# Sum of squared differences by rows: 16 loads in place of 18, larger last pieces of row 7, and that row's squares and sums in PSUM

## The chip, the cores and the metric

The kernel runs on one core of a Trainium2 chip. The metric is the device time of one execution in microseconds; lower is better. A trace is of one execution; the times are medians of several.

## The reference

```python
batch, dim = 1024, 4096
x = np.random.randn(batch, dim).astype(np.float32)
y = np.random.randn(batch, dim).astype(np.float32)

def reference(x, y, axis):          # axis = -1
    return np.sum((x - y) ** 2, axis=axis).astype(np.float32)
```

Two inputs of 16.8 MB each are read once, and 4 KB are written. Each of the 128 partitions holds eight rows of 4096 columns ("row 0" to "row 7"), 32768 columns of x and as many of y.

## The kernel before

The sync engine issues all loads. VectorE subtracts y from x in place, ScalarE squares each piece and sums it in the same instruction, and a small VectorE reduction adds the partial sums of a row. Tensors live in one of two on-chip memories, SBUF (`alloc_sbuf_tensor`) or PSUM (`alloc_psum_tensor`); the kernel before uses SBUF alone. The lists `xw` and `yw` are the widths of the loads, in columns.

```python
xw = [4096, 12288, 8192, 5472, 1280, 960, 320, 160]
yw = [16256, 8192, 2624, 2784, 1344, 480, 480, 288]
late, last = 128, 192          # the last 192 columns of y, then 128 columns of row 3, loaded last of all
LATE = 3
halved = (1, 2, 3, 4)          # pieces of these loads of y are computed in two halves
...
for j, (c0, c1) in enumerate(ys):
    final = j == len(ys) - 1
    wait_loaded(c1, landed_y[j][1])
    for piece in pieces_of(j, c0, c1):
        sub(*piece)                                     # VectorE
        if final:                                       # the late piece of row 3, wholly on VectorE
            nc.vector.tensor_tensor_reduce(..., scalar=parts_of(r, 1), accum_out=results[:, r : r + 1])
            continue
        square(*piece, where[piece])                    # ScalarE, with accum_out
    if j == 4:
        for r in (4, 5, 6):
            complete(r)
complete(7)                                             # VectorE: waits for the last sum of row 7, adds 8 sums
nc.sync.dma_start(out=ov, in_=results)
...
def square(c0, c1, acc):
    a = X[:, home(c0, c1)]
    nc.scalar.wait_ge(diffs, n["diffs"])
    nc.scalar.activation(out=a, in_=a, func=Square, accum_out=acc).then_inc(acts, 1)
```

The first five loads (49024 columns of x and y together) fill the buffers; the other 13 are issued when row 1 has been squared, at 53.4 us, and queue behind them. A square is two instructions on ScalarE: the activation, and an accumulator read that writes the sum.

## Time and profile before

| kernel before | |
|---|---|
| median of 6 runs | 84.18 us (84.02 to 84.40) |
| span of the profiled run | 82.6 us |
| last load landed | 80.25 us |
| store of the results issued | 81.18 us |

All positions below are microseconds from the start of the profiled span. "Landing" is the moment at which a load's semaphore has its last increment; the trace records it.

The final reduction alone, from the groups by form, and the end of VectorE's timeline (start, duration, what):

```profile
L188 DVE TENSOR_REDUCE results<-parts 128x1 f32<-128x8 f32 x1 | 0.2, 161 | 0.0
...
80.95 0.08 DVE L204 DVE_READ_ACCUMULATOR2_ANT results<- 128x1 f32 x1
80.99 0.16 DVE L188 TENSOR_REDUCE results<-parts 128x1 f32<-128x8 f32 x1
```

### The profile page before, as it was taken

What the parts mean: (1) busy time and instruction counts of PE and PEld (TensorE: products, weight loads), DVE (VectorE), ACT (ScalarE), POOL (GpSimd) and SP (SyncE); (2) the same over time, 40 slices, a digit from 0 to 9 for tenths busy, and PEclk for the clock granted to TensorE, in tenths of its full rate; (3) what the DMA queues carried; (4) which work ended last, traced back from release to release, by engine and by line L of the source; (5) the groups of instructions that cost most, each with busy time, mean ns of one, the idle gap of its engine ahead of it and who ended that gap; (6) DMA issues with size and microseconds to landing.
All of it is one profiled execution on the core that took longest, in us unless ns stands there. A gap on an engine that the chain in (4) does not pass through costs nothing.

```text
span 82.6 us, 136 instructions
## 1 busy us (share of the span) xinstructions
DVE 36.8 (45%) x27; ACT 33.4 (40%) x41; POOL 0.2 (0%) x4
## 2 busy tenths in 40 slices
DVE  0000000000000000000299999999189996989992
ACT  3300000000000000000000979889896999899991
POOL 0000000000000000000000000000000000000000
DMA  5998998888999991999599699969979799999960
GB/s 127 389 500 381 595 547 381 381 381 381 504 504 504 504 504 63 441 504 504 254 508 508 286 476 508 476 286 508 423 339 509 339 437 440 426 402 416 395 220 2
DMA packets 2736, 33.56 MB, mean 406 GB/s; under 512 B 432, under 2 KB 1328, under 8 KB 1712
## 3 DMA queue, kind: packets, MB, share of 16 engines
q1 hardware_dynamic: 2736, 33.56, 95.9%
HBM read 33.55 MB, written 0.00 MB: 406 GB/s over the span
## 4 chain that ended last, share of the span: by engine, by line
DMA 63%; SPq 16%; DVE 12%; ACT 4%; issue 1%
DMA Y<-in_y_dram 63%; SPq L108 16%; DVE X L175 11%; ACT X L181 4%; DVE Y L204 0%; DVE results L188 0%; SPq L220 0%; DVE results L204 0%
## 5 line engine op out<-in xcount | busy, mean ns | idle before, releaser
L175 DVE TENSOR_TENSOR X<-X,Y 128x2048 f32<-128x2048 f32 (+10 forms) x21 | 36.2, 1780 | 44.3 <-DMA Y<-in_y_dram 44.3
L181 ACT ACTIVATE X<-X 128x2048 f32<-128x2048 f32 (+9 forms) x20 | 31.2, 1559 | 46.1 <-DVE X L175 46.0
L181 ACT ACTIVATION_READ_ACCUMULATOR X<-X 128x1 f32 x20 | 3.7, 186 | 0.0
L181 ACT ACT_TABLE_LOAD x1 | 1.3, 1283 | 1.4 <-PEq L19 1.4
L188 DVE TENSOR_REDUCE results<-parts 128x1 f32<-128x2 f32 (+2 forms) x4 | 0.4, 152 | 0.0
L204 DVE CUSTOM_DVE_ANT_0 Y<-X,parts 128x128 f32<-128x128 f32 x1 | 0.4, 352 | 0.0
L250 POOL MEMSET const-bfloat16-1.0<- 128x1 bf16 x1 | 0.1, 101 | 0.0
L250 POOL MEMSET const-uint8-127<- 128x1 uint8 x1 | 0.1, 101 | 0.0
L250 POOL MEMSET const-float32-0.0<- 128x1 f32 x1 | 0.1, 98 | 0.2 <-issue 0.2
L250 POOL MEMSET const-float32-1.0<- 128x1 f32 x1 | 0.1, 98 | 0.0
L204 DVE DVE_READ_ACCUMULATOR2_ANT results<- 128x1 f32 x1 | 0.1, 83 | 0.0
## 6 DMA issues: line engine op xcount, KB each, us to landing
Y<-in_y_dram SPq DMA_DIRECT2D x1, 8128.0 KB, 39.0
X<-in_x_dram SPq DMA_DIRECT2D x1, 6144.0 KB, 20.2
X<-in_x_dram SPq DMA_DIRECT2D x1, 4096.0 KB, 48.3
Y<-in_y_dram SPq DMA_DIRECT2D x1, 4096.0 KB, 57.5
X<-in_x_dram SPq DMA_DIRECT2D x1, 2736.0 KB, 13.3
X<-in_x_dram SPq DMA_DIRECT2D x1, 2048.0 KB, 7.1
Y<-in_y_dram SPq DMA_DIRECT2D x1, 1392.0 KB, 19.0
Y<-in_y_dram SPq DMA_DIRECT2D x1, 1312.0 KB, 16.1
```

What stands on the lines that cost most here:

```text
L108: nc.sync.dma_start(out=dst[:, home(c0, c1)], in_=src[:, c0:c1]).then_inc(sem, 16)
L175: nc.vector.tensor_sub(out=a, in0=a, in1=Y[:, home(c0, c1)]).then_inc(diffs, 1)
L181: nc.scalar.activation(out=a, in_=a, func=Square, accum_out=acc).then_inc(acts, 1)
L188: nc.vector.tensor_reduce(out=results[:, r : r + 1], in_=parts_of(r, len(row_parts[r])), axis=mybir.AxisListType.X, op=add,).then_inc(sums, 1)
L204: nc.vector.tensor_tensor_reduce(out=Y[:, home(*piece)], in0=X[:, home(*piece)], in1=X[:, home(*piece)], scale=1.0, scalar=parts_of(r, 1), ...
L250: nc = _bacc.Bacc("TRN2", target_bir_lowering=False, num_devices=1)
```

## The change

The intent: fewer loads, so fewer packets; larger last pieces; and, so that ScalarE can keep up with them, the squares of row 7 (which nobody reads) and its eight sums in PSUM. Five of the six lists and numbers change (`LATE` stays), and the outputs of ScalarE in row 7.

```diff
-    xw = [4096, 12288, 8192, 5472, 1280, 960, 320, 160]
-    yw = [16256, 8192, 2624, 2784, 1344, 480, 480, 288]
-    late, last = 128, 192
+    xw = [4096, 12288, 8192, 5536, 1344, 736, 576]
+    yw = [16288, 8192, 2720, 2816, 1344, 736, 288]
+    late, last = 96, 288
     LATE = 3
-    halved = (1, 2, 3, 4)
+    halved = (1, 2, 3, 4, 5)
...
+    last_parts = nc.alloc_psum_tensor("last_parts", [P, 512], F32).ap()
+    last_squares = nc.alloc_psum_tensor("last_squares", [P, 7 * 512], F32).ap()
+    squares_at = {}
+    k = 0
+    for piece in reversed(row_parts[-1]):
+        w = piece[1] - piece[0]
+        if k + w > 7 * 512:
+            break
+        squares_at[piece] = last_squares[:, k : k + w]
+        k += w
...
     def parts_of(r, m):
-        return parts[:, first[r] : first[r] + m]
+        home_of = last_parts if r == R - 1 else parts
+        return home_of[:, first[r] : first[r] + m]
...
     def square(c0, c1, acc):
...
-        nc.scalar.activation(out=a, in_=a, func=Square, accum_out=acc).then_inc(acts, 1)
+        to = squares_at.get((c0, c1), a)
+        nc.scalar.activation(out=to, in_=a, func=Square, accum_out=acc).then_inc(acts, 1)
```

More of the change, by code (lines that the diff above doesn't have):

```diff
@@ L145 @@
     parts = nc.alloc_sbuf_tensor("parts", [P, total], F32).ap()
+    last_parts = nc.alloc_psum_tensor("last_parts", [P, 512], F32).ap()
+    last_squares = nc.alloc_psum_tensor("last_squares", [P, 7 * 512], F32).ap()
+    squares_at = {}
     k = 0
-    for r, p in enumerate(row_parts):
-        for piece in p:
-            where[piece] = parts[:, k : k + 1] if len(p) > 1 else results[:, r : r + 1]
-            k += len(p) > 1
+    for piece in reversed(row_parts[-1]):
[4 more added lines that the diff above has]
+        k += w
     first = {}
@@ L154 @@
         if len(p) > 1:
-            first[r] = k
-            k += len(p)
+            first[r] = 0 if r == R - 1 else k
+            k += 0 if r == R - 1 else len(p)
     def parts_of(r, m):
-        return parts[:, first[r] : first[r] + m]
+        home_of = last_parts if r == R - 1 else parts
+        return home_of[:, first[r] : first[r] + m]
+    for r, p in enumerate(row_parts):
+        for k, piece in enumerate(p):
+            where[piece] = parts_of(r, len(p))[:, k : k + 1] if len(p) > 1 else results[:, r : r + 1]
     seen_x = [0]
```

## The prediction

> **What bounds the kernel now.** I read the page from the top: busy shares first, then the slices, then the chain, and then the trace in order of time for the last five microseconds.
>
> ```profile
> DVE 36.8 (45%) x27; ACT 33.4 (40%) x41; POOL 0.2 (0%) x4
> ...
> DMA  5998998888999991999599699969979799999960
> ```
>
> Neither engine is busy half of the span, while the DMA row is near full until its last two slices. The transfers bound the kernel, but "DMA-bound" says only when the last bytes land. What follows that landing is the other part of the time.
>
> ```profile
> 66.94 13.12 DMA Y<-in_y_dram
> 80.05 0.02 issue
> 80.08 0.57 DVE X L175 x2
> 80.65 0.03 issue
> 80.67 0.35 DVE Y L204
> 81.03 0.01 DVE results L204
> 81.03 0.12 DVE results L188
> ```
>
> This is the end of the chain that ended last (start, duration, what). The load of the last 192 columns of y lands at 80.05 us. Then come two subtractions (192 and 128 columns), the fused multiply-and-sum of the late 128 columns, and the final reduction. The store is issued at about 81.18 and the span is 82.6. So there are three clocks in the tail: the stream (80.05), VectorE (1.1 us behind it), and ScalarE, which the chain hides. ScalarE's own timeline:
>
> ```profile
> 78.88 0.60 ACT L181 ACTIVATE X<-X 128x480 f32<-128x480 f32 x1
> 79.38 0.19 ACT L181 ACTIVATION_READ_ACCUMULATOR X<-X 128x1 f32 x1
> 79.47 0.59 ACT L181 ACTIVATE X<-X 128x480 f32<-128x480 f32 x1
> 79.97 0.19 ACT L181 ACTIVATION_READ_ACCUMULATOR X<-X 128x1 f32 x1
> 80.08 0.44 ACT L181 ACTIVATE X<-X 128x288 f32<-128x288 f32 x1
> 80.42 0.19 ACT L181 ACTIVATION_READ_ACCUMULATOR X<-X 128x1 f32 x1
> 80.52 0.35 ACT L181 ACTIVATE X<-X 128x192 f32<-128x192 f32 x1
> 80.77 0.19 ACT L181 ACTIVATION_READ_ACCUMULATOR X<-X 128x1 f32 x1
> ```
>
> There is no gap in brackets: ScalarE runs back to back from about 72.9 us to the end. Its last sum is out at 80.77 + 0.19 = 80.96, and the final reduction, which needs it, starts at 80.99. VectorE is free for that reduction at the same 80.99 (accumulator read from 80.95). The two compute engines are **tied** at the end, so a change has to shorten both, or the stream, to win anything.
>
> **What the Trainium skill says.** "DMA: Bandwidth & Descriptors", Specifications, gives a fabric ceiling of 435 GB/s and asks for at least 512 B per transfer for line rate. The first load lands at 7.1 us and the fifth at 60.27 (issue 2.77 + 57.5 to landing). Between them lie 12288 + 16256 + 8192 + 8192 = 44928 columns of 512 B in 53.17 us: 1.183 ns a column, 433 GB/s. The trace agrees; this stream has nothing left to gain but per-load costs. "ScalarE: Activation LUTs", What ACT_TABLE_LOAD costs, gives 186 ns + 0.833 ns per column for an ACTIVATE with immediate operands; the rows above agree (0.60 us at 480, 0.35 at 192). The same page (What happens when an `exp` ACTIVATE runs) calls PSUM the lower-latency port for ScalarE, without a figure. "Perfetto Trace Analysis", Optimizing Scalar/DVE Operations, has it: a data-access overhead of about 93 ns for ScalarE on SBUF against 51 on PSUM, and about 60 against 125 for VectorE, with the write half overlapping the next instruction. No instruction of the kernel before touches PSUM, so this trace can't confirm it. The cited sentence about overlap is what decides this case.
>
> **The change part by part.**
>
> *Stream.* All bytes stay. The 13 loads after the fifth carry 16512 columns, 19.54 us at 1.183 ns, but need 80.2 - 60.27 = 19.97 us (the last 128-column load is issued at 67.4 and takes 12.8). The rest is about 0.033 us for each load. Two loads fewer save 0.07 us. The new final load has 96 columns, 384 B per partition, below the skill's 512 B; it is one load, and I charge nothing beyond the usual for it. The fifth load comes 32 columns later, 0.04 us. Laying the new sizes one after another gives landings of 76.7 (y 1344), 78.5 (y 736), 79.2 (x 576), 79.6 (y 288), 80.0 (y 288) and 80.15 (y 96): the stream ends some 0.07 us sooner, but the load before the last comes at nearly the same time as before.
>
> *VectorE.* From the trace, a subtraction takes 0.155 us + 1.042 ns a column and the next one starts about 0.08 before its end. After 80.0: 288 columns (the next starts 0.375 later), 96 columns (0.255 to its end), 0.03 for the wait, 0.24 to the accumulator read, 0.04 to the reduction: it can start at about 80.97. Before it was 80.99. The tail subtracts 384 columns instead of 320, but multiplies 96 instead of 128. **Nothing won**, about 0.02.
>
> *ScalarE.* Start to start, a square costs 0.20 us + 0.833 ns a column: activation to accumulator read 0.11, read to next activation 0.09. Row 7 had eight squares (640, 672, 672, 672, 480, 480, 288, 192) and still has eight (704, 736, 672, 672, 352, 384, 288, 288), the same 4096 columns. The number of instructions in the tail does not fall; fewer loads are offset by halving the 736 piece. But the last square is now 288 and not 192 wide, 0.08 us longer. I replayed both kernels with these durations, each engine waiting for landings and for the other engine. The replay puts the store of before at 81.19 (measured 81.18). With the new sizes and everything still in SBUF, ScalarE's backlog grows: its last sum comes at about 81.27, the reduction at 81.30, the store at 81.49, that is **0.30 us later**. So the sizes alone lose, and PSUM is there to pay for them.
>
> *PSUM.* Seven of the eight squares of row 7 write their squares there (3392 columns fit in 7 x 512; the first 704 do not), and all eight write their sums there. If the 42 ns (93 - 51) come off start to start, seven squares gain 0.29 us; as ScalarE then catches up and waits for VectorE at the last piece, about 0.27 is felt and the last sum comes at 80.94 to 80.97: level with VectorE, store at 81.17. If the accumulator read gains too, it is off the path by then, and VectorE's 80.97 is the floor. If only the acknowledgement gets shorter and start to start stays, 42 ns once at the end are all: store at 81.45. Last, the final reduction now reads eight sums from PSUM: by the skill up to 65 ns more than the 0.161 us of today. Sum: 84.19 + (81.17 - 81.18) + 0.06 = 84.24 in the good case; 84.19 + 0.27 + 0.06 = 84.5 in the bad one.
>
> **The rivals.** (1) *PSUM does not speed up the chain of squares*: for it, the skill's remark that the write half overlaps, and the 0.09 us overlap seen between every activation and its accumulator read; against it, the 0.11 us from the end of an activation's columns to the accumulator read, which reads no tensor and so looks like a cost of the destination. Time 84.5. I give it 0.4. (2) *PSUM gives the 42 ns or more*: ScalarE stops being tied, VectorE and the stream alone set the end; 84.15 to 84.25. I give it 0.5. (3) *The stream gains more than counted*, because larger packets run better: a view of 1328 packets under 2 KB speaks for it, but per-load costs add up to only 0.43 us in all 13 loads, and half of it would be needed for even 0.2 us. With VectorE in step, 84.0. I give it 0.1. (4) *The 384 B load is slow, or ScalarE's and VectorE's accesses to PSUM get in each other's way.* Against the second: "PSUM — Partial Sum Buffer", PSUM bank collisions, says two engines on one bank at once give an error, not a delay, and here VectorE reads the sums only after ScalarE's last. A slow last load has a slack of 0.25 us, since the 288 subtraction covers it.
>
> **Range and chances.** The two main cases are 84.2 and 84.5; I put the median at 84.25. The runs of before spread from 84.17 to 84.4, so the range is 84.0 to 84.6. All that this change can touch is the last microsecond of 84; 2% is 1.7 us. Chances: faster by over 2%: 0.01, same 0.98, slower 0.01.
>
> **What would show each step.** Landings: the last load at 80.1 to 80.2, with no gap in the DMA row. ScalarE: for an activation into PSUM, a duration near 0.187 + 0.833 ns per column less 42 ns, and, what counts, the distance from one start to the next at equal width (0.20 + 0.833 ns per column today). A small idle time before the 288-column squares would confirm the good case; back-to-back squares to the end with a last sum after 81.2, the bad one. The final reduction: 0.16 against up to 0.23 us. The prediction is wrong if squares into PSUM are slower, if a write across two banks costs extra, or if the stream itself moves by more than 0.2 us.

## More of the kernel before

From the page's parts on DMA and on groups of instructions (line, engine, operation, out<-in, count, then busy time in us and the mean ns of one, then idle time before):

```profile
DMA packets 2736, 33.56 MB, mean 406 GB/s; under 512 B 432, under 2 KB 1328, under 8 KB 1712
...
L181 ACT ACTIVATION_READ_ACCUMULATOR X<-X 128x1 f32 x20 | 3.7, 186 | 0.0
```

## The result, and the profile after

| | before | changed |
|---|---|---|
| median of 6 runs, us | 84.18 | 84.10 (83.99 to 84.39) |
| changed / before | | 0.9995, 95% interval 0.9972 to 1.0018 |
| fifth load landed, us | 60.27 | 60.33 |
| last load landed, us | 80.25 | 80.19 |
| store issued, us | 81.18 | 81.28 |
| span, us | 82.6 | 82.7 |

A ratio is the mean time of one kernel's fast runs over that of the other's fast runs of the same rounds, so it is not quite the ratio of the medians in the table. The two kernels are the same in time. The loads end 0.06 us sooner, and the store leaves 0.10 us later: something in the tail takes back more than the stream gives.

The page of the changed kernel, the same rows as before:

```profile
DVE 36.8 (44%) x27; ACT 33.2 (40%) x41; POOL 0.2 (0%) x4
...
DMA  5999998888999995599699889969989899999950
...
DMA packets 2448, 33.56 MB, mean 406 GB/s; under 512 B 528, under 2 KB 784, under 8 KB 1424
...
L193 ACT ACTIVATION_READ_ACCUMULATOR last_squares<-X 128x1 f32 x7 | 0.9, 129 | 0.0
L200 DVE TENSOR_REDUCE results<-last_parts 128x1 f32<-128x8 f32 x1 | 0.2, 167 | 0.0
```

There are 288 packets fewer and the DMA row is as full as it was. An accumulator read takes 129 ns in place of 186 at the seven squares that go to PSUM (149 at the first square of row 7, whose sum alone goes there). The final reduction, which now reads PSUM, takes 167 ns against 161 before.

The end of the chain that ended last (start, duration, what):

```profile
57.31 22.36 DMA Y<-in_y_dram
79.67 0.02 issue
79.69 0.47 DVE X L186
80.16 0.02 issue
80.19 0.88 ACT last_squares L193 x4
81.06 0.02 issue
81.09 0.17 DVE results L200
```

This is a different chain from that of before. It does not start at the load before the last (landed at 80.03) but one load earlier, at 79.67: 288 columns of y, their subtraction, and then **both** last squares on ScalarE, one after the other. VectorE is done with the late piece before that, as its timeline shows:

```profile
80.72 0.32 DVE L216 CUSTOM_DVE_ANT_0 Y<-X,parts 128x96 f32<-128x96 f32 x1
80.97 0.08 DVE L216 DVE_READ_ACCUMULATOR2_ANT results<- 128x1 f32 x1
81.09 0.17 DVE L200 TENSOR_REDUCE results<-last_parts 128x1 f32<-128x8 f32 x1
```

VectorE reads its accumulator at 80.97 and could reduce soon after; the reduction starts at 81.09, when ScalarE's last sum is there. ScalarE's timeline:

```profile
76.13 0.77 ACT L193 ACTIVATE X<-X 128x704 f32<-128x704 f32 x1
76.81 0.15 ACT L193 ACTIVATION_READ_ACCUMULATOR X<-X 128x1 f32 x1
76.86 0.77 ACT L193 ACTIVATE last_squares<-X 128x736 f32<-128x736 f32 x1
77.57 0.13 ACT L193 ACTIVATION_READ_ACCUMULATOR last_squares<-X 128x1 f32 x1
77.62 0.73 ACT L193 ACTIVATE last_squares<-X 128x672 f32<-128x672 f32 x1
...
80.19 0.41 ACT L193 ACTIVATE last_squares<-X 128x288 f32<-128x288 f32 x1
80.53 0.13 ACT L193 ACTIVATION_READ_ACCUMULATOR last_squares<-X 128x1 f32 x1
80.59 0.41 ACT L193 ACTIVATE last_squares<-X 128x288 f32<-128x288 f32 x1
80.92 0.14 ACT L193 ACTIVATION_READ_ACCUMULATOR last_squares<-X 128x1 f32 x1
```

From an accumulator read to the next activation it is 0.05 us at three places of row 7 (76.81 to 76.86, 77.57 to 77.62, 80.53 to 80.59; 51 ns each in the trace), where it was 0.09 before. At the other four places ScalarE is no longer behind: it waits for VectorE and starts 0.03 us after the subtraction has ended, as here, where the trace has the subtraction from 77.50 to 78.35:

```profile
78.28 0.13 ACT L193 ACTIVATION_READ_ACCUMULATOR last_squares<-X 128x1 f32 x1
78.38 0.73 ACT L193 ACTIVATE last_squares<-X 128x672 f32<-128x672 f32 x1
```

Already the first of the three pairs, whose squares still go to SBUF and whose sum goes to PSUM, shows the 0.05. That pointed to a question that the prediction had not asked: which of the two outputs has to be in PSUM?

### The profile page after: what moved, and what is told of

The parts are those of the page before. It is cut to its first block, busy times and chain, and to the rows that moved or that the text cites. A ratio compares the mean times of both kernels' runs of the same rounds, so it can differ in the third digit from the quotient of the medians.

```text
span 82.7 us, 133 instructions
## 1 busy us (share of the span) xinstructions
DVE 36.8 (44%) x27; ACT 33.2 (40%) x41; POOL 0.2 (0%) x4
## 4 chain that ended last, share of the span: by engine, by line
DMA 74%; DVE 11%; ACT 6%; SPq 5%; issue 1%
DMA Y<-in_y_dram 74%; DVE X L186 11%; SPq L108 5%; ACT X L193 4%; ACT last_squares L193 1%; DVE results L200 0%; SPq L232 0%
## 5 line engine op out<-in xcount | busy, mean ns | idle before, releaser
L186 DVE TENSOR_TENSOR X<-X,Y 128x2048 f32<-128x2048 f32 (+11 forms) x21 | 36.1, 1779 | 44.4 <-DMA Y<-in_y_dram 44.2
L193 ACT ACTIVATE X<-X 128x2048 f32<-128x2048 f32 (+6 forms) x13 | 27.0, 2076 | 46.4 <-DVE X L186 46.3
L193 ACT ACTIVATE last_squares<-X 128x672 f32<-128x672 f32 (+4 forms) x7 | 4.0, 575 | 0.0
L193 ACT ACTIVATION_READ_ACCUMULATOR X<-X 128x1 f32 x13 | 2.4, 183 | 0.0
L193 ACT ACTIVATION_READ_ACCUMULATOR last_squares<-X 128x1 f32 x7 | 0.9, 129 | 0.0
```

The lines of the kernel that those rows point to most:

```text
L186: nc.vector.tensor_sub(out=a, in0=a, in1=Y[:, home(c0, c1)]).then_inc(diffs, 1)
L193: nc.scalar.activation(out=to, in_=a, func=Square, accum_out=acc).then_inc(acts, 1)
```

## The experiments

Ten runs were made, all correct; two of them repeat a kernel. Kernels are compared only within the same rounds. The runs of the kernel before: medians 84.17 and 84.12 us. To keep the stream's scatter out of the comparison, I cut each trace in three: the landing of the fifth load; "stream", from there to the last landing; "tail", from the last landing to the issue of the store. These and the store are from the one trace of each row; the time is a median over several executions, but for the last two rows. All in us:

| kernel | fifth load | stream | tail | store | time, median | ratio to before (95%) |
|---|---|---|---|---|---|---|
| before | 60.27 | 19.99 | 0.93 | 81.18 | 84.18 | |
| changed | 60.33 | 19.87 | 1.09 | 81.28 | 84.10 | 0.9995 (0.9972 to 1.0018) |
| changed, again | 60.48 | 19.87 | 1.06 | 81.41 | 84.18 | 1.0023 (0.9996 to 1.0051) |
| sizes only | 60.37 | 19.87 | 1.16 | 81.39 | 84.15 | 1.0006 (0.9986 to 1.0026) |
| PSUM only | 60.24 | 19.99 | 0.88 | 81.11 | 83.99 | 0.9987 (0.9966 to 1.0007) |
| PSUM only, again | 60.44 | 19.95 | 0.92 | 81.30 | 84.15 | 1.0007 (0.9987 to 1.0027) |
| changed, only sums in PSUM | 60.36 | 20.01 | 1.08 | 81.45 | 84.21 | 1.0003 (0.9988 to 1.0018) |
| changed, only squares in PSUM | 60.41 | 19.90 | 1.13 | 81.44 | 84.25 | 1.0035 (1.0006 to 1.0064) |
| tuned sizes | 60.42 | 20.11 | 0.94 | 81.47 | 84.19 | 1.0010 (0.9994 to 1.0026) |
| x cut in four, tail | 60.57 | 20.72 | 1.04 | 82.33 | 84.91 | 1.0100 (1.0079 to 1.0120) |
| x cut in two, tail | 60.49 | 20.20 | 1.04 | 81.73 | 84.51 | one run, state unknown (before: 83.99) |
| x cut, early | 61.23 | 19.91 | 1.10 | 82.23 | 85.00 | one run, state unknown (before: 83.99) |

From the store to the end of the span it is 1.44 to 1.45 us in every one of them.

**Theory:** the sizes alone lose time in the tail, because ScalarE falls behind; PSUM shortens each square from start to start and wins it back; so the change as a whole is a draw. **Rival:** the fewer, larger loads win by themselves and PSUM does nothing.

### The sizes alone

The edit is against the kernel before, so all of row 7 is in SBUF:

```diff
-    xw = [4096, 12288, 8192, 5472, 1280, 960, 320, 160]
-    yw = [16256, 8192, 2624, 2784, 1344, 480, 480, 288]
-    late, last = 128, 192
+    xw = [4096, 12288, 8192, 5536, 1344, 736, 576]
+    yw = [16288, 8192, 2720, 2816, 1344, 736, 288]
+    late, last = 96, 288
     LATE = 3
-    halved = (1, 2, 3, 4)
+    halved = (1, 2, 3, 4, 5)
```

> The new load sizes (16 loads) with all squares and sums of row 7 in SBUF. Theory: the loads land as in the changed kernel (the load before the last at 80.03 us, the last at 80.19), but the squares cost 0.20 us + 0.833 ns a column from start to start again, so ScalarE runs back to back to the end, its last sum comes at 81.2 to 81.3 and the store is issued at 81.4 to 81.5, some 0.15 to 0.25 us later than in the changed kernel (81.28). Time 84.3 to 84.5. Rival: the larger, fewer loads are a gain by themselves and PSUM adds nothing: store at 81.3 or sooner, time as the changed kernel, 84.1.

Measured: store at 81.39, just under what was expected (the last sum, at 81.17, too), and a tail of 1.16 us, the longest of all. The chain of this kernel ends so:

```profile
73.28 0.02 issue
73.31 7.88 ACT X L181 x22
81.18 0.02 issue
81.20 0.16 DVE results L188
```

For the last 7.9 us nothing but ScalarE stands on the chain: eleven squares and eleven accumulator reads back to back. In its timeline the distances are those of SBUF:

```profile
79.24 0.48 ACT L181 ACTIVATE X<-X 128x352 f32<-128x352 f32 x1
79.62 0.19 ACT L181 ACTIVATION_READ_ACCUMULATOR X<-X 128x1 f32 x1
79.72 0.51 ACT L181 ACTIVATE X<-X 128x384 f32<-128x384 f32 x1
...
80.99 0.19 ACT L181 ACTIVATION_READ_ACCUMULATOR X<-X 128x1 f32 x1
```

From 79.24 to 79.72 it is 0.48 us for 352 columns, 0.187 us over the 0.833 ns a column. In the trace the mechanism is as the theory has it. But the time, 84.15 against 84.17 for before, misses the low end of what I expected by more than a tenth and is near what the rival had said (its store, at 81.3 or sooner, did not come): the loss of 0.2 us in the trace is no larger than the scatter between runs, and the ratio (1.0006) does not show it.

### PSUM alone

```diff
-    xw = [4096, 12288, 8192, 5536, 1344, 736, 576]
-    yw = [16288, 8192, 2720, 2816, 1344, 736, 288]
-    late, last = 96, 288
-    halved = (1, 2, 3, 4, 5)
+    xw = [4096, 12288, 8192, 5472, 1280, 960, 320, 160]      # the old sizes, row 7 in PSUM
+    yw = [16256, 8192, 2624, 2784, 1344, 480, 480, 288]
+    late, last = 128, 192
+    halved = (1, 2, 3, 4)
```

> The old load sizes (18 loads), with the squares and sums of row 7 in PSUM. Theory: ScalarE gets free of its backlog (last sum at 80.87 in place of 80.96), but VectorE still reaches the final reduction only at 80.98, so the store stays at 81.15 to 81.20 and the time within 0.05 us of before. Rival: ScalarE alone had set the end, then the store comes at 81.08 or sooner.

Measured: tail 0.88 against 0.93, store at 81.11, of which 0.03 is an earlier fifth load. Its VectorE at the end, and ScalarE's last read:

```profile
80.71 0.13 ACT L193 ACTIVATION_READ_ACCUMULATOR last_squares<-X 128x1 f32 x1
```

```profile
80.64 0.35 DVE L216 CUSTOM_DVE_ANT_0 Y<-X,parts 128x128 f32<-128x128 f32 x1
80.92 0.08 DVE L216 DVE_READ_ACCUMULATOR2_ANT results<- 128x1 f32 x1
80.92 0.16 DVE L200 TENSOR_REDUCE results<-last_parts 128x1 f32<-128x8 f32 x1
```

ScalarE's last sum is out at 80.84, 0.08 us ahead of the reduction, which now waits for VectorE alone, and starts together with VectorE's accumulator read (in the second trace too, at 81.11), not 0.04 us after it. So the tie of before was not exact: VectorE was by that measure free at 80.95, and the reduction at 80.99 came 0.03 us after ScalarE's last sum, the same 0.03 as in the changed kernel (81.06 to 81.09), where ScalarE is clearly last. With the old sizes PSUM frees ScalarE and takes off these 0.04 us, no more, since VectorE stays where it was: from the landing of the load before the last, on which VectorE's chain hangs, to the reduction it is 0.94 us before, and 0.89 and 0.90 in the two traces of PSUM alone. The store at 81.11 lies between what the theory (81.15 to 81.20) and the rival (81.08 or sooner) had said. The ratio, 0.9987, has an interval that contains 1.

### Which output has to be in PSUM

Only the sums:

```diff
-        to = squares_at.get((c0, c1), a)
+        to = a
```

> The changed kernel, but the squares of row 7 go back to SBUF; only their sums are in PSUM. Theory A (the place of the sum counts: the next activation starts 0.05 us after an accumulator read into PSUM, 0.09 after one into SBUF): start to start stays 0.144 us + 0.833 ns a column, the store stays within 0.04 us of the changed kernel's 81.28, time as the changed kernel. Theory B (the place of the squares counts): start to start goes back to 0.20 us and the store to 81.4 to 81.5, as with the sizes alone.

Only the squares:

```diff
-        home_of = last_parts if r == R - 1 else parts
+        home_of = row7 if r == R - 1 else parts      # row7: 512 columns of SBUF
```

> The changed kernel, but the sums of row 7 go back to SBUF; only the squares are in PSUM. Theory A (the place of the sum counts): accumulator read to next activation is 0.09 us again, start to start 0.19 to 0.20 us + 0.833 ns a column, store at 81.4 to 81.5. Theory B (the place of the squares counts): start to start as in the changed kernel, store at 81.28 to 81.34.

Timeline of ScalarE with only the sums in PSUM (the trace gives an accumulator read the names of its activation's tensors, not where the sum goes):

```profile
77.71 0.15 ACT L193 ACTIVATION_READ_ACCUMULATOR X<-X 128x1 f32 x1
77.76 0.76 ACT L193 ACTIVATE X<-X 128x672 f32<-128x672 f32 x1
...
80.67 0.15 ACT L193 ACTIVATION_READ_ACCUMULATOR X<-X 128x1 f32 x1
80.72 0.44 ACT L193 ACTIVATE X<-X 128x288 f32<-128x288 f32 x1
```

The same, with only the squares there:

```profile
77.66 0.19 ACT L193 ACTIVATION_READ_ACCUMULATOR last_squares<-X 128x1 f32 x1
77.75 0.72 ACT L193 ACTIVATE last_squares<-X 128x672 f32<-128x672 f32 x1
...
80.61 0.19 ACT L193 ACTIVATION_READ_ACCUMULATOR last_squares<-X 128x1 f32 x1
80.70 0.40 ACT L193 ACTIVATE last_squares<-X 128x288 f32<-128x288 f32 x1
```

With the sums in PSUM the next activation follows an accumulator read after 0.05 us; with the squares there and the sums in SBUF, after 0.09, as before the change. The squares in PSUM make the activation itself shorter in the record (0.72 against 0.76 for 672 columns), but what follows starts no sooner. The place of the sum counts. With the sums alone ScalarE is held by VectorE at most squares, as in the changed kernel, so the short gap is seen freely only at the first pair shown (before the second, the subtraction ended 0.03 us before the activation started); with the squares alone every gap of row 7 is 92 ns or more. The tails agree: 1.08 with the sums alone, as the whole change (1.09, 1.06), and 1.13 with the squares alone, near the sizes alone (1.16).

A tail also moves with the landing of the last load, which follows the one before it after 0.16 to 0.20 us in these traces. Counted from the landing of the 288 columns on which the changed kernel's chain hangs (79.67 there) to the final reduction, it is 1.42 and 1.42 us in the two traces of the change, 1.45 with the sums alone, and 1.51 with the squares alone as with the sizes alone. Of the 0.03 us between 1.42 and 1.45, 0.02 is the last accumulator read: with the squares in SBUF it takes 153 ns, with both in PSUM 135 (128 at most others). So the squares in PSUM do shorten a read whose sum goes there too, but on the path this counts once.

The store of the kernel with the sums alone came at 81.45, not within 0.04 of 81.28 as expected: its last load landed 0.17 us later (80.36 against 80.19). Theory A therefore rests on the gaps and the tails, not on the store or the time. The ratio with the squares alone, 1.0035, is the one of these whose interval lies above 1; two of its six runs (84.71 and 84.84) make most of that, and its tail does not explain 0.3 us.

### What a load costs the stream

```diff
-    xw = [4096, 12288, 8192, 5536, 1344, 736, 576]
+    xw = [4096, 12288, 8192] + 4 * [1384] + 4 * [336] + 4 * [184] + 4 * [144]      # cut in four: 28 loads
```

> The changed kernel with its last four loads of x each cut in four: 28 loads in place of 16, the same bytes. It measures what a load costs the stream. Theory (0.033 us a load, from the sum of the landings of before): 12 more loads move the last landing from 80.2 to about 80.6 us, and the two loads that the change saves are worth 0.07 us. Rival (packets are what counts, larger ones run better): with 12 x 128 packets more it comes at 81 or later. Second rival (a load costs nothing, the scatter of the stream is larger): 80.2 to 80.35.

```diff
-    xw = [4096, 12288, 8192, 5536, 1344, 736, 576]
+    xw = [4096, 12288, 8192] + 2 * [2768] + 2 * [672] + 2 * [368] + 2 * [288]      # cut in two: 20 loads
```

> The changed kernel with its last four loads of x each cut in two: 20 loads, 4 more. Cutting them in four (12 more) took the stream after the fifth load from 19.87 to 20.72 us, 0.07 us a load. If the cost is per load, the stream is 20.15 us here; at the 0.03 to 0.04 us a load that the change itself showed, 20.0.

```diff
-    xw = [4096, 12288, 8192, 5536, 1344, 736, 576]
+    xw = [4096] + 6 * [2048] + 8 * [1024] + [5536, 1344, 736, 576]      # early loads cut: 28 loads
```

> The changed kernel with two early loads of x (12288 and 8192 columns) cut into 6 of 2048 and 8 of 1024: 28 loads, 12 more, all of 4 KB or more a partition. If a load costs the same at any size, 0.07 us, the first subtractions' y and the fifth-to-last early landing come later by 0.85 us in all: the last early load lands at 61.2 to 61.3 in place of 60.33 to 60.48. If only small pieces cost, it stays at 60.3 to 60.6. The stream after it stays at 19.87 either way.

Twelve more loads in the tail took 0.85 us of stream (20.72 - 19.87), four more took 0.33 (20.20, where 20.15 was expected for a cost per load), twelve more of 4 KB and larger, early, moved the fifth of the former landings by 0.75 to 0.90 us (61.23 against 60.33 and 60.48; 61.2 to 61.3 was expected for a cost per load): 0.06 to 0.08 us a load, for loads of 0.6 to 11 KB a partition in the tail and of 4 and 8 KB early. Two of the three are single runs of unknown state. The two cuts of the tail change one thing more than the number of loads: the first smaller loads fit into the space of row 0, so they are issued at 49 us, 4 us sooner than in the changed kernel. The pages of the two kernels with 28 loads have the same number of packets, first the cut tail, then the cut early loads:

```profile
DMA packets 4176, 33.56 MB, mean 401 GB/s; under 512 B 720, under 2 KB 2512, under 8 KB 3280
```

```profile
DMA packets 4176, 33.56 MB, mean 401 GB/s; under 512 B 720, under 2 KB 976, under 8 KB 2640
```

They cost about the same although one has 2512 packets under 2 KB and the other 976. So it is the number of packets (or loads, which these runs do not part), not their being small. Of my three expectations for the first run the rival from packets held by its number: the last load landed at 81.29 (60.57 + 20.72), and 81 or later was its sign. But its reason, that larger packets run better, is not what the second pair of pages shows. The cost is twice the theory's 0.033 us.

This leaves a gap. At 0.07 us a load, two loads fewer and 32 columns already landed should shorten the stream by 0.18 us; five traces of the new sizes have 19.87, 19.87, 19.87, 19.90 and 20.01, against 19.99, 19.99 and 19.95 with the old sizes, so some 0.1 us less in most. Why removing two gives less per load than adding four or twelve costs is open.

### Other sizes

```diff
+    xw = [4096, 12288, 8192, 4992, 512, 1312, 960, 416]
+    yw = [16320, 8192, 3168, 2336, 1312, 416, 544, 192]
+    late, last = 64, 224
+    halved = (1, 2, 4, 6)
```

> Other sizes with the sums and squares of row 7 in PSUM, found by replaying the tail with measured durations: 18 loads, the last 224 columns of y and a late piece of 64. Replay: VectorE free at 80.85, the last sum at 80.93, store at 81.12 against 81.17 with the old sizes and PSUM, and 81.28 measured for the change: 0.05 to 0.15 us sooner than the change, that is 0.1%. If the replay misses a wait, 81.2 to 81.3.

A miss. The tail is 0.94, as short as with the old sizes, but the stream took 20.11, so the store came at 81.47. The replay saw no harm in 18 loads; but the old sizes have 18 loads too and a stream of 19.95 to 19.99, so the number of loads does not explain the 20.11. What does was not tested.

### The change and PSUM alone, again

> The old sizes with row 7 in PSUM, a second time, beside the changed kernel on one chip. Theory: from the last landing to the store it takes 0.88 to 0.90 us again, against 1.09 for the change, so it is the faster of the two by 0.05 to 0.2 us (the change has two loads fewer, 0.07 us). Rival: the change gains as much in the stream, and the two are equal.

> The changed kernel once more. Theory: within 0.1 us of before; from the last landing to the store 1.05 to 1.10 us. If it is over 0.2 us faster or slower than before, the scatter from run to run is larger than what the parts do.

On one chip, the tails came out as 0.92 and 1.06, the streams as 19.95 and 19.87. PSUM alone had the better tail again, by 0.14 (though 0.92 is over the 0.88 to 0.90 expected), and lost 0.08 of it in the stream. The times are 84.15 and 84.18 us beside 84.12 for before: none of the three can be told from the others. The fifth load landed at 60.24 to 60.48 us in these kernels without added loads; that scatter, before the tail has begun, is larger than anything that the change does.

## Why the prediction was right

The predicted time was 84.25 us and the range 84.0 to 84.6; measured were 84.10 and, again, 84.18. The range took in the good case and the bad one, so the time says little of the mechanism. By its steps:

1. **The stream is the bound and can win only per-load costs: right, the size was off.** The predicted landings held within 0.1 us (76.7, 78.5, 79.2, 79.6, 80.0 and 80.15 against 76.70, 78.55, 79.30, 79.67, 80.03 and 80.19). The 0.033 us for a load was read from sums of landings in one trace; loads added on purpose cost 0.06 to 0.08.
2. **VectorE gains nothing: right, in part by luck.** It was to be free at 80.97; its accumulator read began at 80.97. The working had the read at 80.93 and added 0.04 to the reduction; the read came 0.04 later, and PSUM alone shows that the 0.04 is not there. So the reading of before as a tie was off by as much: VectorE was free at 80.95, ScalarE set the 80.99.
3. **The sizes alone lose 0.30 us: right in kind, too large.** Measured were 0.21 us to the store (81.39 against 81.18). The step that was mis-sized is the 0.20 us of a square beyond its columns. I had taken it from a kernel whose ScalarE looked back to back, because its timeline shows no idle time in brackets, but which still waited a few ns for VectorE at several squares (that of 78.11 started 34 ns after its subtraction had ended, and took 0.204 from start to start). A ScalarE that is really behind takes 0.187, and so do two squares of the trace of before (75.89 to 76.61 and 76.61 to 77.35: 0.187 and 0.185 us over 0.833 ns a column).
4. **PSUM takes 42 ns off seven squares from start to start: right in the size, wrong in the place and the count.** Where ScalarE is free to start, 0.09 became 0.05 us, but at three places of row 7, not seven. And the step argued from where the squares go. The runs showed that the sum's destination does it, and the squares' destination does not. I had taken the 0.11 us in front of the accumulator read for the cost of the destination, and put a gain of the read itself aside as off the path; the gain was behind the read. That the size fits is luck as far as the squares go.
5. **ScalarE is then level with VectorE, the store comes at 81.17: wrong by 0.1 us.** PSUM won back 0.11 us by the stores of one trace each (81.39 to 81.28), 0.09 from the landing at 79.67 on (1.51 to 1.42), not 0.27. ScalarE was to catch up only at the last piece; it had caught up at the square of 78.38, and from there VectorE's subtractions held it at four of the five last squares. Less had been lost, too, and the last two squares of 288 columns are a chain of their own behind the load that landed at 79.67. That load came 0.07 us later than my laying-out had it, and with two wide squares behind it there is no slack. ScalarE sets the end by 0.1 us.
6. **The reduction pays up to 65 ns for PSUM: wrong.** This was an estimate from the page's 125 and 60 ns, and the sum took 0.06 us of it; measured were 167 ns against 161.

The errors of 5 and 6 have opposite signs and half cancel, so the trace's store was 0.05 us later than in the good case with the charge (81.23), and within the scatter. That is luck, not a working that came true. The chance of 0.98 for "same" rested on the tail being the last microsecond of 84, which every run bears out.

Of the rivals, (1) fell with the 0.05 us gaps, though for the squares by themselves it holds; of (2) the 42 ns came, but VectorE and the stream did not set the end, ScalarE did. (3) had some truth in it, a load costs more than I counted, but the change removes only two. On (4), the last load of 384 B landed 0.16 to 0.20 us after the one before it in the traces with the new sizes, the one of 512 B 0.17 to 0.20 with the old: no penalty is seen beyond that scatter.

## What to carry to other kernels

When two engines and a transfer end within 0.1 us of one another, a change that helps one of them moves the time by no more than its lead over the next (here 0.04 us); find the second and third in line before counting a gain. On a chain of many short activations with sums, try the **sums** in PSUM first: one small tensor gave all of the change's gain between squares, and the large one for the squares gave 0.02 us at most, at the last read. And compare tails from the last landing on, not from the start of the span, if the stream before them scatters more than the effect.

## What the Trainium skill lacked or had wrong

- "ScalarE: Activation LUTs", Step-by-step: what each stage is for, calls PSUM the lower-latency port for an ACTIVATE's destination. The record of an activation is shorter indeed (672 columns: 0.72 against 0.76 us), but the next instruction starts no sooner. The page lacks what an accumulator read costs: 186 ns into SBUF and 128 into PSUM (153 where the squares stay in SBUF), with 92 to 94 and 50 or 51 ns from its start to the next activation where nothing else is waited for. None of the pages that I read has this.
- "Perfetto Trace Analysis", Optimizing Scalar/DVE Operations, gives 93 ns on SBUF and 51 on PSUM for ScalarE. These two numbers appear, within 1 ns, as the gap behind an accumulator read, and they follow where that read *writes*; the same section says that the write half overlaps with the next instruction. From an activation to its accumulator read, beyond the columns, no such difference is seen: 92 ns with two squares of 672 columns in SBUF (sizes alone), 92 and 93 with them in PSUM (squares alone).
- The same section gives 60 against 125 ns for VectorE on SBUF and PSUM. The final reduction of eight sums took 161 ns from SBUF and 167 from PSUM: a difference of 65 ns is not seen.
- "DMA: Bandwidth & Descriptors", Specifications, asks for 512 B a transfer. A last load of 384 B a partition landed 0.16 to 0.20 us after the one before, one of 512 B 0.17 to 0.20: no penalty beyond the scatter. No page that I read gives what one more load of 128 partitions costs a full queue issued by the sync engine; here it was 0.06 to 0.08 us, for added loads of 4 and 8 KB a partition and for those of 0.6 to 11 KB alike.
